# A Mamba-2 and sliding-window-attention trunk on one core: group 3's queries ahead of output block 1, the residual's scaling in the key/value block, and no transpose of probabilities on TensorE

## The chip, the cores and the metric

The kernel runs on one core of a Trainium2 chip. The metric is device time in microseconds (us) of one execution. The core's engines each work through an instruction queue of their own: TensorE (PE in the profile, its weight loads PEld), VectorE (DVE), ScalarE (ACT), GpSimd (POOL) and SyncE (SP, which here only issues transfers). They wait for each other by semaphores.

## The reference

A trunk of two layers on 256 tokens of width 2048, in float32. The first is a Mamba-2 mixer, the second an attention layer; each is followed by `LayerNorm(alpha * x + mixer(x))`. The change touches the second layer only:

```
k, v = _shared_kv(x, kv_w, kv_b, cos, sin)      # 4 heads of 64, rotary on 16 of 64
proj = x @ w_in                                  # queries (32 heads) | gate
q = rope(proj[..., :Q_WIDTH] + q_bias);  gate = proj[..., Q_WIDTH:]
s = where(valid, q k^T / 8, -inf)                # window of 128 tokens
m = max(max(s), sink)
p = exp(s - m) / (sum(exp(s - m)) + exp(sink - m))
o = (p v) * silu(gate)
out = LayerNorm(alpha * x + o @ w_out)
```

## The kernel before, in words

All large products are made in three matmuls each, from operands split into a high and a low part (`wh`, `wl` for weights, `x1H`, `x1L` for activations). Weights come in *units* of 128 x 2048, in two halves: SP loads a half into a raw buffer (`wr`, `load_half`, six buffers), ACT rounds it to `wh` (`split_half`, L163) and DVE subtracts to get `wl` (L166). Six `wh` and four `wl` buffers keep this some units ahead of PE.

The attention layer works on two halves `h` of 128 tokens and four *groups* `j` of eight heads, one key/value head each. Its stages, in the order of `B_ORDER`, are blocks of four units:

- the key/value block (L982 to L1017): `x_stat` (matmul at L975) for `h` = 0 and then, with the same four units, for `h` = 1. DVE adds the bias (L1001, L1005) and turns the keys by `rope`, POOL doubles them (L1007), PE transposes them (`ktr`, L1012).
- `q_block(j)`: 24 matmuls a unit (L975); behind the fourth unit DVE adds the bias (L1055) and does the `rope` (L960 to L965) for both halves. `qtr` transposes them on PE (L1061), and ACT copies them to `qT` (L1065).
- `gate_block(j)`: 48 matmuls a unit (L251); ACT and DVE make the gate `sg` (L1081, L1082).
- the output block `("o", j)`: `out_unit`, 24 matmuls a unit (L322 to L324); DVE adds each result to the residual `xr` (L329, L333).

Small work is hung between units. `later(n, fn)` puts `fn` on a list, and `tick()`, called behind each unit of these blocks, counts down and calls what is due; such a place on PE's queue is called a *visit* here. `tick` calls what is due in the order in which it was put on the list. `attend(j, h)` makes the scores (L1114 for `h` = 0, L1121 for `h` = 1), masks them (L1129, or ACT's copies L1134 with DVE's predicated copies L1137), takes the maximum (L1145), the exponentials on ACT (L1151) and the scale (L1157). Then the probabilities have to be turned. `turn_far` does it by a transpose of 32 x 32 blocks on DVE (L1170), copies on ACT (`moved`, L1179; ten for `h` = 0, sixteen for `h` = 1) and, for `h` = 1, two masks on DVE (`parts`, L1186). `turn_p` does it by eight transposes on PE (L1199) and four masked copies on DVE (L1205); only (j, h) = (3, 1) takes that way. `pv` makes the products with the values (L1231 for `h` = 0; L1245 and L1252 for `h` = 1), DVE multiplies by the gate (L1219), ACT and DVE split the result (L1259, L1260) for the output block.

The residual needs the first layer's normalization with gain and bias. `residual(c, h)` does it for a block of 512 columns: a multiply (L1028) and an add (L1029) on DVE, with gain and bias loaded by POOL (`load_affine`, L1023) into one pair of buffers. The eight calls are hung on visits 1 to 14 (`RES_AT`), the loads of the later blocks on `GB_AT`.

A scheduler puts the instructions of the engines in order when the program is built; where `keep_in_program_order` is asked for, it keeps the order of the code. What is built is fixed: each engine takes its queue in that order.

## Time and profile before

| what | us |
|---|---|
| median of 3 runs | 992.03 (991.72 to 992.22) |
| the profiled execution's own time | 992.29 |
| its span, first to last instruction | 990.3 |
| PE busy | 979.4 |
| DVE busy | 781.1 |
| ACT busy | 599.4 |
| POOL busy | 103.5 |
| mean granted TensorE clock | 0.999 |

The rows shown below are lines of the profile's views. A row of a timeline has start and duration in us, engine, line and operation, the tiles written and read, how many instructions are merged in it, and in brackets the engine's idle time before it and what ended that. A row of the chain has start, us and what. A row of the waits has the engine and line that waited, for whom, us in total, how often, and the longest. A row of windows has the window, its length, the busy time and count of PE, PEld, DVE, ACT and POOL, the granted clock, the DMA share and GB/s. Line numbers are those of the kernel before. The attention layer's stages run from about 661 us (key/value block) over 686 (query block 0) to 953 (last unit of output block 2), and its end to 990.

### The profile page before, as it was taken

To read this page: it belongs to the slowest core of one execution; us is meant where nothing else is said; L and a number is where in the kernel's file an instruction comes from. 1 tells how busy PE (TensorE), PEld (TensorE's weight loads), DVE (VectorE), ACT (ScalarE), POOL (GpSimd) and SP (SyncE) were. 2 spreads that over 40 slices of the span, in tenths; PEclk is the share of its full clock that TensorE was granted. 3 is DMA by queue.
4 is the path that set the end of the run, shared out by engine and by line. 5 is a ranking of instruction groups with operands and counts; after the bars stand their busy time and mean duration, and the time that the engine had idled before them with its cause. 6 is when DMAs were issued, how large, how long until landed. Compare 5 with 4: busy or idle time off the path is not lost.

```text
span 990.3 us, 18070 instructions
## 1 busy us (share of the span) xinstructions
PE 979.4 (99%) x7076; PEld 892.2 (90%) x7076; DVE 781.1 (79%) x1211; ACT 599.4 (61%) x1076; POOL 103.5 (10%) x133
## 2 busy tenths in 40 slices
PE   9999999999999999999999999999999999999998
PEld 8999989999999998999999999888898888988976
DVE  7888896867786887686787687889678878687796
ACT  7585866547646654664664664566477575674652
POOL 0001303004003002100300300302000000000003
PEclk9999999999999999999999999999999999999999
DMA  9788577575576666656657466456755557547532
GB/s 362 254 278 310 170 262 220 173 236 171 194 235 187 217 209 195 202 186 209 202 175 237 141 205 213 152 178 217 236 169 175 164 160 239 151 152 219 184 108 85
DMA packets 61557, 198.89 MB, mean 201 GB/s; under 512 B 6849, under 2 KB 11361, under 8 KB 61217
## 3 DMA queue, kind: packets, MB, share of 16 engines
q1 hardware_dynamic: 58528, 188.53, 58.9%
q0 software_dynamic: 2336, 8.69, 2.9%
q8 instruction: 55, 0.90, 0.4%
q10 hardware_dynamic: 608, 0.52, 0.2%
q14 instruction: 30, 0.24, 0.1%
HBM read 195.49 MB, written 2.23 MB: 200 GB/s over the span
## 4 chain that ended last, share of the span: by engine, by line
PE 92%; DVE 4%; ACT 2%; issue 1%; DVEq 0%; ACTq 0%
PE mm L251 50%; PE mm L975 9%; PE mm L322 9%; PE mm L323 8%; PE mm L324 8%; PE ax L630 2%; DVE wl L166 1%; ACT p L1151 1%; PE ax L606 1%; ACT pt L1179 0%; PE mm L389 0%; PE ax L589 0%; ACT wh L163 0%; PE ax L906 0%; PE ax L1114 0%
## 5 line engine op out<-in xcount | busy, mean ns | idle before, releaser
L166 DVE TENSOR_TENSOR wl<-wr,wh 128x1024 fp32r<-128x1024 f32 (+2 forms) x338 | 393.5, 1184 | 99.9 <-ACT wh L163 96.5
L163 ACT ACTIVATE wh<-wr 128x1024 fp32r<-128x1024 f32 (+2 forms) x338 | 331.2, 1010 | 154.8 <-issue 51.4
L251 PE MATMUL mm<-xH,wh 128*128 128x256 f32 x1280 | 356.1, 278 | 0.0
L251 PE MATMUL mm<-xL,wh 128*128 128x256 f32 x1280 | 354.6, 277 | 0.0
L251 PE MATMUL mm<-xH,wl 128*128 128x256 f32 x1280 | 354.5, 277 | 0.0
L251 PEld LDWEIGHTS mm<-xH,wh 128*128 128x128 f32 x1280 | 240.8, 188 | 2.0 <-issue 0.5
L251 PEld LDWEIGHTS mm<-xL,wh 128*128 128x128 f32 x1280 | 240.7, 188 | 1.0
L251 PEld LDWEIGHTS mm<-xH,wl 128*128 128x128 f32 x1280 | 240.5, 188 | 0.0
L322 PE MATMUL mm<-wh,yH 128*128 128x512 f32 x256 | 101.5, 397 | 0.0
L323 PE MATMUL mm<-wh,yL 128*128 128x512 f32 x256 | 99.9, 390 | 0.0
L324 PE MATMUL mm<-wl,yH 128*128 128x512 f32 x256 | 99.9, 390 | 0.0
L646 POOL TENSOR_TENSOR yz<-yz,z 128x256 f32<-128x256 f32 x32 | 32.5, 1024 | 468.6 <-DVE yz L641 468.6
L251 PE MATMUL mm<-x1H,wh 128*128 128x256 f32 x256 | 71.9, 281 | 0.0
L493 DVE SCALAR_TENSOR_TENSOR cv<-mm,pc,cv 128x255 f32<-128x255 f32 x144 | 68.7, 477 | 3.3 <-ACT cv L491 1.9
L251 PE MATMUL mm<-x1H,wl 128*128 128x256 f32 x256 | 71.1, 278 | 0.0
L251 PE MATMUL mm<-x1L,wh 128*128 128x256 f32 x256 | 71.1, 278 | 0.0
L975 PE MATMUL mm<-wh,x1H 128*128 128x512 f32 x160 | 63.0, 394 | 0.0
L975 PE MATMUL mm<-wl,x1H 128*128 128x512 f32 x160 | 61.9, 390 | 0.0
L975 PE MATMUL mm<-wh,x1L 128*128 128x512 f32 x160 | 60.9, 390 | 0.0
L322 PEld LDWEIGHTS mm<-wh,yH 128*128 128x128 f32 x256 | 48.1, 188 | 10.3 <-DVE z L582 0.9
L324 PEld LDWEIGHTS mm<-wl,yH 128*128 128x128 f32 x256 | 48.1, 188 | 10.1
L331 DVE SCALAR_TENSOR_TENSOR xr<-mm,r,xr 128x512 f32<-128x512 f32 x64 | 47.1, 745 | 11.7 <-PE mm L324 7.4
(226 smaller groups left out, 1373.1 us busy)
## 6 DMA issues: line engine op xcount, KB each, us to landing
wr<-in_wa SPq DMA_DIRECT2D x154, 512.0 KB, 5.1
wr<-in_wo SPq DMA_DIRECT2D x64, 512.0 KB, 4.5
wr<-in_wq SPq DMA_DIRECT2D x32, 512.0 KB, 4.0
wr<-in_wg SPq DMA_DIRECT2D x31, 512.0 KB, 4.9
wr<-in_wb SPq DMA_DIRECT2D x16, 512.0 KB, 4.7
wr<-in_wb SPq DMA_DIRECT2D x32, 256.0 KB, 3.7
rb<-rscr SPq DMA_DIRECT2D x11, 512.0 KB, 4.1
wr<-in_wkv SPq DMA_DIRECT2D x8, 512.0 KB, 5.0
```

Source lines behind the costliest of these rows:

```text
L163: m = nc.scalar.activation(h[:, sl], v, AF.Copy)
L166: m = nc.vector.tensor_tensor(l[:, sl], v, h[:, sl].bitcast(F32), ALU.subtract)
L251: m = nc.tensor.matmul(ps, a, b, start=first and i == 0, stop=last and i == 2)
L322: pinned(nc.tensor.matmul(ps, aH[:, k, hs], u.h[:, ks], start=k == 0 and add is None, stop=False), pin)
L323: pinned(nc.tensor.matmul(ps, aL[:, k, hs], u.h[:, ks], start=False, stop=False), pin)
L324: pinned(nc.tensor.matmul(ps, aH[:, k, hs], u.l[:, ks], start=False, stop=k == 3), pin)
L331: nc.vector.scalar_tensor_tensor(v, ps, rms[:, h : h + 1], v, ALU.mult, ALU.add)
L493: nc.vector.scalar_tensor_tensor(a[:, sft:], ps[:, : S - sft], w(3 - sft), a[:, sft:], ALU.mult, ALU.add)
L606: nc.tensor.transpose(ps[:, o : o + P], st.xs[i][:, c * P : (c + 1) * P], ident)
L630: nc.tensor.matmul(ps[64 * r : 64 * r + 64, cols], xd[:, c, r, :], e[:, 256:] if c else e[:, :256], start=c == 0, stop=c == 1,)
L646: nc.gpsimd.tensor_tensor(v, v, st.z[i][:], ALU.mult)
L975: m = nc.tensor.matmul(ps[:], (x1H, x1L, x1H)[i][:, kk, hs], (u.h, u.h, u.l)[i][:, ks], start=(kk, i) == (0, 0), stop=ui == 3 and (k, i) = ...
```

## The change

Five edits, all in the second layer.

1. `B_ORDER`: query block 3 stands before output block 1, which was ahead of it.
2. `turn_p` is gone. Scores (3, 1) take `turn_far` as all others do, and `attend(3, 1)` comes three visits behind `attend(3, 0)`, not one.
3. `PV_AT` and `MASK_AT` are lists per group. The query transposes are put at the head of the list (`place`), the masks too; the first product comes in the visit of the query transposes of the next group, the second in the visit of its first scores, ahead of them.
4. `residual` and `load_affine` move: the first block's gain and bias are loaded during the key/value block's first unit, the second's during its fourth, the third's and fourth's right behind each half, all in buffers of their own. Three residuals are called in the second half of the key/value block, five on visits 0 to 4.
5. In `rope` the last add, in `residual` the multiply and in `parts` both masks keep the order of the code.

Visits are counted from the first unit of query block 0. What hangs on them, before and after (turn = transpose of queries, S = scores, M = masks, V = products with the values):

```
before: 4 turn 0; 5 S00; 8 S01; 12 M01, turn 1; 13 V00 V01 S10; 16 S11; 20 M11; 21 V10 V11;
        24 turn 2; 25 S20; 28 S21; 32 M21; 33 V20 V21; 36 turn 3; 37 S30; 38 S31; 41 turn_p; 42 V30 V31
after:  4 turn 0; 5 S00; 8 S01; 12 turn 1, M01 V00; 13 V01 S10; 16 S11; 22 M11; 24 turn 2, V10;
        25 V11 S20; 28 S21; 32 turn 3, M21 V20; 33 V21 S30; 36 S31; 40 M31; 41 V30 V31
```

The diff, cut to its core:

```
-B_ORDER = [("q", 0), ("g", 0), ("q", 1), ("g", 1), ("o", 0), ("q", 2), ("g", 2), ("o", 1),
-           ("q", 3), ("g", 3), ("o", 2), ("o", 3)]
-RES_AT = [2, 3, 6, 7, 11, 12, 14, 15]
-MOVE_AT, MASK_AT = [2, 2, 3, 3], 4
-PV_AT = [[8, 5], [5, 4]]
-GB_AT = [0, 4, 8, 13]
+B_ORDER = [("q", 0), ("g", 0), ("q", 1), ("g", 1), ("o", 0), ("q", 2), ("g", 2), ("q", 3),
+           ("o", 1), ("g", 3), ("o", 2), ("o", 3)]
+MOVE_AT, MASK_AT = [2, 2, 3, 3], [4, 6, 4, 4]
+GB_AT = {0: 0, 3: 1}
+PV_AT = [[7, 5], [11, 9], [7, 5], [8, 5]]
...
-    def later(n, fn):
-        pending.append([n, fn])
+    def later(n, fn, place=None):
+        pending.insert(len(pending) if place is None else place, [n, fn])
...
+    def load_affine(c):
+        if c:
+            t = bp.tile([P, 1024], F32, tag="own" if c == 1 else "p", name=nm("gb1"), bufs=1 if c == 1 else 3)
+            gb1[c] = t[:, :512], t[:, 512:]
+        else:
+            gb1[c] = [bp.tile([P, 512], F32, tag=f"gb{i}", name=nm("gb1"), bufs=1)[:] for i in range(2)]
+        for v, n in zip(gb1[c], ("lng", "lnb")):
+            nc.gpsimd.dma_start(v, A[n][0, c * 512 : (c + 1) * 512].partition_broadcast(P))
...
+                if ui in GB_AT:
+                    load_affine(GB_AT[ui])
+            elif ui:
+                residual(ui // 3, 1 if ui == 2 else 0)
...
+        if h == 0:
+            load_affine(2)
+    load_affine(3)
+    for n in range(1, 6):
+        later(n, lambda n=n: residual((n + 2) // 2, (n + 2) % 2))
...
-            later(1, qtr)
+            later(1, qtr, h)
...
-                    nc.vector.tensor_tensor(d, t, masked(kc, 8), ALU.mult)
+                    tc.keep_in_program_order(nc.vector.tensor_tensor(d, t, masked(kc, 8), ALU.mult))
...
-                later(MASK_AT, parts)
+                later(MASK_AT[j], parts, 0)
...
-        def turn_p():
...
-        if far:
-            turn_far()
-        else:
-            later(3, turn_p)
-        later(PV_AT[j == 3][h], pv)
+        turn_far()
+        later(PV_AT[j][h], pv)
         if h == 0:
-            later(1 if j == 3 else 3, lambda: attend(j, 1))
+            later(3, lambda: attend(j, 1))
```

The built queues of the changed kernel in the stretch from scores (2, 1) on, in order (w = half a weight unit, named by block and unit; xr = output sum; S, M, V, turn as above):

```
DVE: ... S21 copies, maximum | S21 scale, w o1.1, transpose, w o1.1, w o1.2, bias and rope of query half 0,
     bias and four rope products of half 1, w o1.2, last two rope operations, w o1.3, xr, w o1.3, xr,
     first M21, gate V20, second M21, low V20, w g3.0, xr, w g3.0, xr, w g3.1, gate V21, w g3.1, low V21,
     S30 mask and maximum, xr, xr | xr, S30 scale, w g3.2, transpose, xr, w g3.2, w g3.3 (2), w o2.0, gate,
     S31 copies, w o2.0, maximum | gate, S31 scale, w o2.1, transpose, w o2.1, w o2.2, gate, gate, w o2.2,
     xr, w o2.3 (2), xr, first M31, w o3.0, second M31, ...
ACT: ... S21 exponentials, w o1.1 (2), w o1.2, 16 copies, w o1.2, w o1.3 (2), w g3.0, queries 3 (2), w g3.0,
     V20, w g3.1 (2), V21, S30 exponentials, w g3.2 (2), w g3.3 (2), 10 copies, w o2.0, gate, w o2.0,
     S31 copies, S31 exponentials, gate, w o2.1 (2), w o2.2, 8 copies, gate, 8 copies, gate, w o2.2, w o2.3 (2), ...
```

More of the change, by code (lines that the diff above doesn't have):

```diff
@@ L964, in rope @@
         nc.vector.tensor_tensor(x1, a, b, ALU.subtract)
-        nc.vector.tensor_tensor(x2, d, e, ALU.add)
+        tc.keep_in_program_order(nc.vector.tensor_tensor(x2, d, e, ALU.add))
     def x_stat(ps, h, u, ui, pin=False, last=None):
@@ L979, in x_stat, with residual @@
             pinned(m, pin)
+    gb1 = {}
+    def load_affine(c):
[6 more added lines that the diff above has]
+            nc.gpsimd.dma_start(v, A[n][0, c * 512 : (c + 1) * 512].partition_broadcast(P))
+    def residual(c, h):
+        v = xr[:, h, c * 512 : (c + 1) * 512]
+        tc.keep_in_program_order(nc.vector.tensor_tensor(v, v, gb1[c][0], ALU.mult))
+        nc.vector.tensor_tensor(v, v, gb1[c][1], ALU.add)
     kT = bp.tile([P, 4, S], F32, tag="kT", name="kT")
@@ L1017, in trunk @@
         later(2, ktr)
-    def load_affine(c):
-        for i, n in enumerate(("lng", "lnb")):
-            gb1[i] = bp.tile([P, 512], F32, tag=f"gb{i}", name=nm("gb1"), bufs=1)
-            nc.gpsimd.dma_start(gb1[i][:], A[n][0, c * 512 : (c + 1) * 512].partition_broadcast(P))
-    def residual(c, h):
-        v = xr[:, h, c * 512 : (c + 1) * 512]
-        tc.keep_in_program_order(nc.vector.tensor_tensor(v, v, gb1[0][:], ALU.mult))
-        nc.vector.tensor_tensor(v, v, gb1[1][:], ALU.add)
-    gb1 = {}
-    load_affine(0)
-    for c in range(4):
-        if c:
-            later(GB_AT[c], lambda c=c: load_affine(c))
-        for h in range(2):
-            later(RES_AT[2 * c + h], lambda c=c, h=h: residual(c, h))
+        if h == 0:
[3 more added lines that the diff above has]
+        later(n, lambda n=n: residual((n + 2) // 2, (n + 2) % 2))
     qT = {}
@@ L1099, in attend @@
         p = bp.tile([P, 1024], F32, tag="p", name=nm("p"), bufs=3)
-        far = j < 3 or h == 0
-        byhead = p[:].rearrange("p (c r b) -> p r c b" if far else "p (r c b) -> p r c b", r=8, c=4)
+        byhead = p[:].rearrange("p (c r b) -> p r c b", r=8, c=4)
         per = 512 // nk
@@ L1190, in turn_far @@
             if h:
-                later(MASK_AT, parts)
-        def turn_p():
-            for kc in range(2):
-                pts[kc] = bp.tile([P, 4, 8, 32], F32, tag=("pri", "own")[kc], name=nm("pt"), bufs=1)
-            for par in range(2):
-                pt = ax_tile()
-                for a in range(4):
-                    nc.tensor.transpose(
-                        pt[:, a * P : (a + 1) * P], p[:, (par * 4 + a) * P : (par * 4 + a + 1) * P], ident
-                    )
-                got = blocks(pt[:].rearrange("p (a q) -> p a q", a=4))
-                for kc in range(2):
-                    t = pts[kc][:].rearrange("p c r b -> p r c b")[:, par * 4 : par * 4 + 4]
-                    nc.vector.tensor_tensor(t, got, masked(kc, 4), ALU.mult)
+                later(MASK_AT[j], parts, 0)
         def pv():
```

## The prediction

> **What bounds the kernel now.** I read the page first, then who waited for whom on TensorE (PE) from 690 us on, the chain of work that ended last, and the timelines of VectorE (DVE), ScalarE (ACT) and GpSimd (POOL).

> ```profile
> PE 979.4 (99%) x7076; PEld 892.2 (90%) x7076; DVE 781.1 (79%) x1211; ACT 599.4 (61%) x1076; POOL 103.5 (10%) x133
> PE ax L1061 <- DVE qt L965: 2.0, 1, 2.0
> PE ax L1199 <- DVE p L1157: 1.7, 1, 1.7
> PE ax L1114 <- DVE o L1219: 1.3, 1, 1.3
> ```

> PE is the bound. In the attention half it waits three times, 5.0 us in all, and never for a weight. So an edit is worth something only if it takes work off PE, ends one of these waits or makes a new one. What PE's blocks take, from the chain (start, us, what):

> ```profile
> 697.41 10.90 PE mm L975 x48
> 708.31 5.46 PE mm L251 x48
> 713.77 0.87 PE ax L1061 x8
> 720.11 1.09 PE ax L1114 x16
> 863.92 1.46 PE ax L1121 x32
> 892.84 1.01 PE ax L1231 x4
> 893.85 0.86 PE ax L1245 x8
> 894.72 0.59 PE ax L1252 x8
> 944.90 1.06 PE ax L1199 x8
> 953.90 0.43 PE mm L322
> 954.33 0.23 PE mm L323
> ```

> A query or output unit is 24 matmuls, 5.45 us; a gate unit 48, 5.46. The first matmul behind a visit takes 0.43 in place of 0.23, so a visit costs 0.2 beside its own work.

> **What the change gives.** *No turn on TensorE:* eight transposes at 0.11 (0.87 for eight) go, with 0.1 of the visit's edge: 0.95. Their wait, 1.7, goes too. A wait is counted from the modelled end of the last matmul, some 0.16 behind where the next could start (0.27 for one transpose against 0.11 from start to start), so I add 0.16 to each: 1.86.

> *Residual moved.* DVE and POOL around the old and the new place:

> ```profile
> 757.06 0.68 DVE L1028 TENSOR_TENSOR xr<-xr,gb 128x512 f32<-128x512 f32 x1
> 762.13 1.22 DVE L166 TENSOR_TENSOR wl<-wr,wh 128x1024 fp32r<-128x1024 f32 x1
> 763.40 0.22 DVE L965 TENSOR_TENSOR qt<-rt 128x64 f32<-128x64 f32 x1
> 773.28 0.68 DVE L1219 TENSOR_TENSOR o<-ax,sg 128x512 f32<-128x512 f32 x1
> 675.06 1.63 POOL L1091 MEMSET pt<- 32x256 f32 x3 [11.93 <-DVE x1L L923]
> 686.12 0.42 DVE L1001 TENSOR_TENSOR kd<-mm,bias 128x256 f32<-128x256 f32 x1
> 688.68 1.93 POOL L1007 COPY kd<-kd 128x256 f32<-128x256 f32 x1 [0.98 <-DVE kd L965]
> 696.54 0.87 PE ax L1012 x8
> ```

> The wait of L1061 (2.0, so 2.16) stood behind four of DVE's multiplies and adds since the scores (0.60 each from start to start) and half a weight unit (1.13) between the last rope operations. In the new order all five are gone from there: L965 ends at 763.6 - 2.4 - 1.1 = 760.1, and PE asks at 761.6. So 2.16 goes. In its new place the scaling puts L1001 about 2 us later (part of the multiplies and adds stand ahead of it, some in gaps), so the key copy ends at 692.6; PE asks at 696.5. That, and DVE's 2 us on weights, for which PE doesn't wait, I cost at 0; without the cover it would be 2. Six loads move ahead of POOL's memset and key copies, 0.54 us of issue each by the kernel before, 3.2 in all: the 11.93 of idle time ahead of the memset hides them. On SP's queue eight loads of output block 1 change places with eight of query block 3; a load of this size lands 4 us after its issue:

> ```profile
> wr<-in_wq SPq DMA_DIRECT2D x32, 512.0 KB, 4.0
> ```

> Both blocks' loads are issued as buffers come free, three units ahead of use (16 us): 0.

> *Shared visits:* the first product of a group goes into the visit of the query turns, and the second comes ahead of the next scores. The product visits of groups 1 and 2 are no longer visits of their own: 2 x 0.2 = 0.4. For group 0 the wait of L1114 (1.3, so 1.46) shrinks: ahead of DVE's L1219 four multiplies and adds (2.4) and half a unit (1.1) go, so it stands at 773.3 - 3.5 = 769.8 and ends at 770.4; PE asks at 770.0, so 0.35 is left and 1.1 goes.

> Together: 0.95 + 1.86 + 2.16 + 0.4 + 1.1 = 6.5 us.

> **What it costs.** Group 3's queries now stand before output block 1, and scores (3,1) go the long way: DVE transpose, sixteen copies on ACT, two masks on DVE. PE takes its matmuls in program order, so it waits at the visit that comes too early. How long the path takes, from group 2 as it is:

> ```profile
> 867.77 1.17 ACT L1134 COPY p<-ax 128x256 f32<-128x256 f32 x4
> 874.98 0.21 ACT L1149 ACTIVATE sm<-sm 128x8 f32<-128x8 f32 x1 [2.97 <-DVE sm L1148]
> 881.96 6.66 ACT L1179 COPY pt<-z 32x256 f32<-32x256 f32 x16 [0.84 <-DVE z L1170]
> 868.87 2.48 DVE L1137 COPY_PREDICATED p<-cc,ax 64x128 f32<-64x128 uint32 x8
> 880.09 0.68 DVE L333 TENSOR_TENSOR xr<-xr,mm 128x512 f32<-128x512 f32 x1
> 883.55 2.35 DVE L166 TENSOR_TENSOR wl<-wr,wh 128x1024 fp32r<-128x1024 f32 x2
> 888.65 1.23 DVE L1186 TENSOR_TENSOR pt<-pt,cc 128x1024 f32<-128x1024 f32 x1 [2.15 <-ACT pt L1179]
> 890.93 1.22 DVE L1186 TENSOR_TENSOR pt<-pt,cc 128x1024 f32<-128x1024 f32 x1
> 920.60 1.28 DVE L1129 TENSOR_TENSOR p<-ax,cc 128x512 f32<-128x512 f32 x2
> 924.79 0.49 ACT p L1151 x2
> 932.47 2.90 ACT L1179 COPY pt<-z 32x256 f32<-32x256 f32 x7 [1.17 <-DVE z L1170]
> ```

> Scores at 863.92, copies from 881.96 (18.0 later), second mask at 892.15: 28.2 us. From start to start DVE takes 1.13 for half a weight unit (L166) or a mask, 0.60 for an output sum (L333); ACT 0.415 a copy, 1.0 for a weight half. Now the changed kernel's queues in their new order; 0 is where PE starts scores (2,1).

> 1. Copies start at 18.04 less three output sums (1.8), which are no longer there, and with one weight half more (1.13): 17.4. Sixteen take until 24.0. Behind them on ACT stands the second half of output block 1's third unit, and behind that on DVE the last two rope operations of the queries (3, second half): 24.0 + 1.1 + 1.2 + 0.35 = 26.7. PE asks at 1.46 + 96 matmuls (21.8) + 0.2 + 0.44 = 23.9. **New wait: 2.8.**
> 2. DVE then works off what gathered before it gets to scores (3,0): six weight halves (6.9), four output sums (2.4), two masks (2.3), the products and their low halves (2.4): 40.7.
> 3. From L1129 to the copies 11.9 as at 920.60 to 932.47, by the new order 11.6: 52.3.
> 4. Ten copies (4.15); on ACT a weight unit and a gate before the scores (3,1), which PE made at about 54: 58.7. Masked copies 2.5 and half a unit 1.1 on DVE, the maximum and small ones 1.8: exponentials at 64.4. From there to the copies 7.7 (924.79 to 932.47 in group 3 now): 72.1.
> 5. Sixteen copies with two gates among them (7.4), a weight half on ACT (1.1): 80.6. In DVE's order now stand: half a unit, sum, two halves, sum, mask, half, mask: 4 x 1.13 + 2 x 0.60 + 1.13 + 1.22 = 8.1: **88.7**.

> PE without a wait would ask for the second mask at: 216 matmuls at 0.227 (49.0), 192 gate matmuls at 0.114 (21.9), small blocks 1.46 + 0.8 + 1.0 + 1.5 + 1.1 + 1.46 + 1.0 = 8.3, edges 1.0: **80.2**. So 8.5 us of waiting arise between, however they are split (2.8 at the turns, about 0.7 for accumulators that DVE reads late, 5 at the products of group 3). These hops have an error of some 2 us together. The nearest rows bound it: at least 0 (a path of 28.2 as in group 2 would fit into the 29.9 that PE leaves from scores (3,1) to its products), at most 11 (with two more weight halves ahead).

> Sum without the clock: 992.29 - 6.5 + 8.5 = 994.3 against the profiled execution, 0.26 above the median of 992.03; so 994.0.

> *The clock:*

> ```profile
> 983.57 1.99 PE L1342 MATMUL ax<-t,dg 128*128 128x256 f32 x6
> 985.00:988.00 3.00, 0.56 (x2) 0.00 (x0) 2.03 (x4) 0.69 (x2) 0.00 (x0) 1.00 0.79 293
> 988.00:990.30 2.30, 0.00 (x0) 0.00 (x0) 0.00 (x0) 0.00 (x0) 0.00 (x0) 0.51 0.22 74
> 1.00 2.96 PE L371 MATMUL ax<-zero 128*128 128x512 bf16 x7 [1.00 <-DVE zero L359]
> 4.96 0.34 PE L251 MATMUL mm<-xL,wh 128*128 128x256 f32 x1
> ```

> The last matmul ends at 985.6, and from 988 the granted clock is 0.51: under 2.5 us of rest were enough. At the start six and a half widths of 512 take 2.96, 0.46 each against 0.23: half speed, until the matmuls quicken at about 4.96, 4 us after the first. So a drop costs at most half of 4, 2.0, and at least 0. A rest of 5 us is likely to bring one; the waits of 2 us of before brought none. I take 1.5, nearer the row with the drop. **995.5.** A drop at the first wait costs nothing, since the path above sets the later end.

> [...]

> **Rivals.** (a) *Masks of (3,1) in time, faster.* If DVE is not as far behind as step 2 says, the path of (3,1) takes group 2's 28.2 against 29.9, and only 2.8 at the turns stays: 992.0 - 6.5 + 2.8 = 988.3. It decides once the second mask ends before 82. For it: group 2 was just as full and made it. Against: now output sums and eight halves stand between, and scores (3,0) are only three units ahead. (b) *Neither wait:* 985.5. (c) *Half of it:* a path shorter by 2 to 4 us, no drop: 990 to 993. (d) *Waits, but the clock stays:* 994.0; for it, rests are split by the accumulators. (e) *More late than this:* weights behind the copies on ACT too, 998 and above; against it, weights come 7 us and more ahead in most units, by the lack of any wait for them.

> **How the numbers follow.** Forecast with the drop 0.36, (d) 0.2, (a) 0.19, (b) 0.07, (c) 0.11, (e) 0.07. The likeliest has its own range of 993.5 to 998; with (a) it reaches down to 987, with (d) and (c) between; (b) and (e) mostly stay out: 987.0 to 998.5. About 0.2%, 2 us, is what can be told from no change: faster than 990.0 is (a) and (b), 0.25; within 990.0 to 994.0 (c) and a half of (d), 0.21; slower 0.54.

> **What would show it.** L1199 gone, L1061's wait of group 1 gone, L1114's under 0.5. New: PE waiting at the turns of query block 3 for the last rope operation, 2 to 3 us, behind L166 and the sixteen copies; and at the second product of group 3 for the mask, 4 to 6 us; granted clock under 1.00 just behind it. No wait of PE in the key/value block. I am wrong if DVE ends the masks of (3,1) before PE asks, or if PE waits for weights.

## The result, and the profile after

| | us, median | lowest to highest | ratio to before |
|---|---|---|---|
| before | 992.21 | 991.72 to 993.79 (5 runs) | |
| after | 1001.89 | 1000.41 to 1003.89 (5 runs) | 1.0096, 95% interval 1.008 to 1.0112 |

The change costs about 9.7 us. The profiled execution of the changed kernel took 1001.16, its span is 999.4. Line numbers are from here on those of the changed kernel unless said otherwise: the key copy on GpSimd (POOL) is L1028, the residual's multiply and add are L996 and L997, the transposes of the keys L1033, the copy of the turned keys on ScalarE L1036, the query transposes L1067, the masks L1191, the matmuls of query and key units L974, those of output units L321 to L323, group products with both halves of the keys L1236, rope L959 to L964, the weight halves L162 (ScalarE, ACT) and L165 (VectorE, DVE).

TensorE (PE) from 660 us on, "who waited for whom" (what waited, what for: us in all, times, longest):

```profile
PE ax L1236 <- DVE pt L1191: 3.9, 1, 3.9
PE ax L1033 <- POOL kd L1028: 3.3, 1, 3.3
PE ax L1067 <- DVE qt L964: 2.8, 1, 2.8
PE mm L321 <- DVE sm L1151: 0.4, 1, 0.4
```

The three waits of before are gone (those at L1061 for group 1, at L1114 and at L1199 in that kernel's lines). Three others stand in their place, and a small one for accumulators. The first and the third row were forecast, with about 5 and 2.8; the second, 3.3 us at the transposes of the keys, was forecast not to be there. The chain of what ended last, by stretches around the three (start, us, what):

```profile
693.89 6.46 POOL kd L1028
...
700.39 0.66 PE ax L1033 x4
701.04 7.11 PE mm L974 x24
...
892.57 0.15 DVE qt L964
...
892.85 1.08 PE ax L1067 x4
...
953.47 1.23 DVE pt L1191
...
954.84 1.98 PE ax L1236 x8
```

Behind the first wait 24 matmuls take 7.11 us; before, 48 took 10.90, so 24 should take 5.45. They are slow for 3.4 us of it, from 701.69 on. The stretches of the granted clock, by windows (window: length, then busy us of each engine with the number of its instructions, granted clock, DMA share, GB/s):

```profile
698.28:701.69 3.41, 1.30 (x8) 1.17 (x9) 1.80 (x3) 0.61 (x2) 2.06 (x1) 1.00 0.84 276
701.69:705.10 3.41, 3.41 (x10) 2.62 (x9) 2.41 (x3) 0.93 (x1) 0.00 (x0) 0.50 0.56 185
...
889.42:892.83 3.41, 0.66 (x5) 0.37 (x4) 1.62 (x4) 3.37 (x5) 0.00 (x0) 1.00 0.04 14
892.83:896.25 3.42, 3.40 (x9) 1.48 (x10) 3.42 (x5) 3.19 (x6) 0.00 (x0) 0.50 0.76 206
...
950.86:954.27 3.41, 0.05 (x2) 0.00 (x0) 3.41 (x4) 2.92 (x3) 0.00 (x0) 1.00 0.90 258
954.27:957.69 3.42, 2.85 (x16) 1.16 (x16) 3.42 (x6) 0.15 (x2) 0.00 (x0) 0.50 0.70 227
```

Each of the three waits is followed by 3.41 us at half the clock. Half of what PE works in it is lost: 1.7, 1.7 and, as PE still rests for 0.57 of the third, 1.4 us. The kernel before had no such stretch: its granted clock was 1.00 from 5 to 985 us.

Where the first wait comes from stands in the timelines of GpSimd, VectorE and ScalarE (start, us, engine, line, operation; in brackets idle time before and what ended it):

```profile
678.89 0.72 POOL L1028 COPY kd<-kd 128x256 f32<-128x256 f32 x1 [2.08 <-DVE kd L964]
...
690.72 9.62 POOL L1028 COPY kd<-kd 128x256 f32<-128x256 f32 x1 [0.98 <-DVE kd L964]
```

```profile
690.46 0.19 DVE L964 TENSOR_TENSOR kd<-rt 128x32 f32<-128x32 f32 x1
690.56 0.69 DVE L996 TENSOR_TENSOR xr<-xr,gb 128x512 f32<-128x512 f32 x1
691.17 1.22 DVE L165 TENSOR_TENSOR wl<-wr,wh 128x1024 fp32r<-128x1024 f32 x1
...
699.12 0.96 DVE L165 TENSOR_TENSOR wl<-wr,wh 128x768 fp32r<-128x768 f32 x1
702.66 1.23 DVE L165 TENSOR_TENSOR wl<-wr,wh 128x1024 fp32r<-128x1024 f32 x1 [2.58 <-ACT wh L162]
```

```profile
701.08 0.59 ACT L1036 COPY kT<-ax 128x512 f32<-128x512 f32 x1 [3.00 <-PE ax L1033]
701.57 1.06 ACT L162 ACTIVATE wh<-wr 128x1024 fp32r<-128x1024 f32 x1
```

The second key copy starts at 690.72, just when the prediction had it (692.6 less 1.93). But it takes 9.62 us, not 1.93, and ends at 700.34, 0.26 behind VectorE's last instruction (699.12 + 0.96 = 700.08). VectorE had run without a gap all that time, on instructions that read two inputs from SBUF. The kernel before shows the same thing on a smaller scale, in its own lines (its key copy is L1007; the second one's row, 688.68 with 1.93, stands in the prediction):

```profile
678.77 1.33 POOL L1007 COPY kd<-kd 128x256 f32<-128x256 f32 x1 [2.08 <-DVE kd L965]
...
688.52 1.23 DVE L166 TENSOR_TENSOR wl<-wr,wh 128x1024 fp32r<-128x1024 f32 x1
689.66 0.69 DVE L1028 TENSOR_TENSOR xr<-xr,gb 128x512 f32<-128x512 f32 x1
690.39 0.77 DVE L1029 TENSOR_TENSOR xr<-xr,gb 128x512 f32<-128x512 f32 x1
```

That copy ended at 690.61. The border between L166 and L1028, at 689.7, had not let it in; the first gap, the 0.04 us between multiply and add (689.66 + 0.69 = 690.35 to 690.39), did, and it ended 0.26 behind the gap's start. In the changed kernel weight pieces stand between multiplies and adds, and there is no such gap.

And the three engines closed a circle: VectorE ran dry because ScalarE's next weight half (L162 at 701.57) stood behind the copy of the turned keys (L1036), which waited for PE's transposes, which waited for GpSimd's copy, which had to wait until VectorE ran dry.

### The profile page after: what moved, and what is told of

The parts are those of the page before. It is cut to its first block, busy times and chain, and to the rows that moved or that the text cites. A ratio compares the mean times of both kernels' runs of the same rounds, so it can differ in the third digit from the quotient of the medians.

```text
span 999.4 us, 18069 instructions
## 1 busy us (share of the span) xinstructions
PE 983.4 (98%) x7068; PEld 892.4 (89%) x7068; DVE 783.2 (78%) x1210; ACT 606.3 (61%) x1092; POOL 109.1 (11%) x133
## 4 chain that ended last, share of the span: by engine, by line
PE 89%; DVE 4%; ACT 2%; issue 2%; DMA 1%; POOL 1%; DVEq 0%; SPq 0%; ACTq 0%; POOLq 0%
PE mm L250 51%; PE mm L974 8%; PE mm L321 8%; PE mm L322 8%; PE mm L323 8%; PE ax L629 2%; ACT pt L1184 1%; DVE wl L165 1%; DMA wr<-in_wb 1%; PE ax L605 1%; DVE p L1142 1%; POOL kd L1028 1%; ACT p L1156 1%; ACT wh L162 1%; PE ax L1236 1%
## 5 line engine op out<-in xcount | busy, mean ns | idle before, releaser
L165 DVE TENSOR_TENSOR wl<-wr,wh 128x1024 fp32r<-128x1024 f32 (+2 forms) x338 | 392.7, 1183 | 102.8 <-ACT wh L162 101.0
L162 ACT ACTIVATE wh<-wr 128x1024 fp32r<-128x1024 f32 (+2 forms) x338 | 331.5, 1010 | 148.8 <-PE mm L250 53.3
L321 PE MATMUL mm<-wh,yH 128*128 128x512 f32 x256 | 101.4, 396 | 0.0
L322 PE MATMUL mm<-wh,yL 128*128 128x512 f32 x256 | 99.8, 390 | 0.0
L323 PE MATMUL mm<-wl,yH 128*128 128x512 f32 x256 | 99.7, 389 | 0.0
L974 PE MATMUL mm<-wh,x1H 128*128 128x512 f32 x160 | 63.4, 396 | 0.0
L974 PE MATMUL mm<-wl,x1H 128*128 128x512 f32 x160 | 62.4, 393 | 0.0
L974 PE MATMUL mm<-wh,x1L 128*128 128x512 f32 x160 | 61.6, 394 | 0.0
L321 PEld LDWEIGHTS mm<-wh,yH 128*128 128x128 f32 x256 | 48.1, 188 | 10.3 <-DVE z L581 1.0
L323 PEld LDWEIGHTS mm<-wl,yH 128*128 128x128 f32 x256 | 48.1, 188 | 10.2
## 6 DMA issues: line engine op xcount, KB each, us to landing
wr<-in_wa SPq DMA_DIRECT2D x154, 512.0 KB, 5.0
wr<-in_wo SPq DMA_DIRECT2D x64, 512.0 KB, 4.4
wr<-in_wq SPq DMA_DIRECT2D x32, 512.0 KB, 4.6
wr<-in_wg SPq DMA_DIRECT2D x31, 512.0 KB, 4.8
wr<-in_wb SPq DMA_DIRECT2D x16, 512.0 KB, 4.3
rb<-rscr SPq DMA_DIRECT2D x11, 512.0 KB, 4.1
wr<-in_wkv SPq DMA_DIRECT2D x8, 512.0 KB, 4.7
```

What stands on the lines that cost most here:

```text
L162: m = nc.scalar.activation(h[:, sl], v, AF.Copy)
L165: m = nc.vector.tensor_tensor(l[:, sl], v, h[:, sl].bitcast(F32), ALU.subtract)
L321: pinned(nc.tensor.matmul(ps, aH[:, k, hs], u.h[:, ks], start=k == 0 and add is None, stop=False), pin)
L322: pinned(nc.tensor.matmul(ps, aL[:, k, hs], u.h[:, ks], start=False, stop=False), pin)
L323: pinned(nc.tensor.matmul(ps, aH[:, k, hs], u.l[:, ks], start=False, stop=k == 3), pin)
L974: m = nc.tensor.matmul(ps[:], (x1H, x1L, x1H)[i][:, kk, hs], (u.h, u.h, u.l)[i][:, ks], start=(kk, i) == (0, 0), stop=ui == 3 and (k, i) = ...
```

## The experiments

**1. The key copy on ScalarE.** Theory A: GpSimd is kept out of SBUF by VectorE's gapless run.

```
-        nc.gpsimd.tensor_copy(kd[:, :, 1, :], kd[:, :, 0, :])
+        (nc.scalar.copy if h else nc.gpsimd.tensor_copy)(kd[:, :, 1, :], kd[:, :, 0, :])
```

> The changed kernel with one edit: the second key copy (L1028, second half of the rows) runs on ScalarE instead of GpSimd; nothing else moves. Theory A (GpSimd's read of SBUF is locked out while VectorE runs instructions with two SBUF inputs without a gap, since the moved residual fills VectorE's gaps): the copy then ends by about 692, PE's 3.3 us wait at the visit of the keys goes, and so does the half-clock stretch of 3.41 us behind it (1.7 us): 1001.9 - 3.5 - 1.7 = 996.7 us. Rival B (the keys themselves are late, because the residual pushes VectorE's bias and rope back): the copy starts as late as before and PE still waits 3 us or more: 1001 to 1002. Rival C (the wait is hidden by the later waits anyway, because the masks of group 3 set the end): the wait goes, the later ones grow by as much: 1000 or above.

Measured: 997.12 (996.44 to 997.48). The wait and the half-clock stretch behind it are gone (mean clock of the profiled run 0.997, 0.995 in the changed kernel's), 4.8 us in all; the other two waits stand as they were (4.0 and 2.9). That fits A. The keys were not late (B), and the later waits did not take the gain back (C).

**2. The residual later, the copy left on GpSimd.**

```
     for n in range(1, 6):
-        later(n, lambda n=n: residual((n + 2) // 2, (n + 2) % 2))
+        later(n + 2, lambda n=n: residual((n + 2) // 2, (n + 2) % 2))
```

> The changed kernel with one edit: the five residual steps that stand in query block 0 come two visits later (third to seventh visit in place of first to fifth); the three in the key/value block and the copy on GpSimd stay. Theory A (GpSimd locked out by a gapless VectorE): VectorE has gaps again behind the key's rope, the 9.6 us copy falls to 1 to 2 us, PE's wait and the clock drop behind it go: about 996.7, plus 0 to 1.5 if the later residual now delays the first queries' rope: 996 to 998.5. Rival (the copy is slow because of what GpSimd itself does: the loads and the bias issue in its queue): copy still 9 to 10 us, time 1001 to 1002.

Measured: 997.04 (996.33 to 998.18). The copy takes 5.41, not 1 to 2, since VectorE now does five weight pieces without a gap; but it ends before PE asks. GpSimd's row, and VectorE's:

```profile
691.23 5.41 POOL L1028 COPY kd<-kd 128x256 f32<-128x256 f32 x1 [0.97 <-DVE kd L964]
```

```profile
691.08 4.70 DVE L165 TENSOR_TENSOR wl<-wr,wh 128x1024 fp32r<-128x1024 f32 x5
695.69 0.68 DVE L996 TENSOR_TENSOR xr<-xr,gb 128x512 f32<-128x512 f32 x1
696.41 0.77 DVE L997 TENSOR_TENSOR xr<-xr,gb 128x512 f32<-128x512 f32 x1
```

The copy ends at 696.64. The first gap in VectorE's run is the 0.04 us between L996 and L997 (695.69 + 0.68 = 696.37 to 696.41): L997 adds to what L996 has just written. The copy ends 0.27 behind that gap's start, and L997 took 0.77 in place of 0.68. So what lets the copy in need not be an idle engine: a gap of 0.04 us was enough, here as in the kernel before.

**3. Group 3's second products one visit later.**

```
-PV_AT = [[7, 5], [11, 9], [7, 5], [8, 5]]
+PV_AT = [[7, 5], [11, 9], [7, 5], [8, 6]]
```

> The changed kernel with one edit: the second value products of group 3 one visit later (six visits behind their scores in place of five). Theory A (the long way of the masks is what the second product waits for, 3.9 us, and half clock for 3.41 us follows): the wait and the drop go and nothing takes their place, as the last output block asks for the result about 11 us later: 1001.9 - 4.1 - 1.7 = 996.1. Rival B (the work behind is late anyway, so a wait appears at the start of the last output block or in the final normalization): 1000 or above. Rival C (wait goes, clock drop stays for another reason): 997.8.

Measured: 995.26 (994.04 to 1001.02, 8 runs). The wait of 3.9 is gone and nothing takes its place; the work behind it has about 10 us to spare (the second half's result is ready at 966.2; the last output block asks for it behind its four units of the first half, at about 976, an estimate from 48 matmuls of 0.23), so B falls. Its runs spread by 7 us, and they follow the mean granted clock: 994.04 and 994.09 at 1.0, 1001.02 at 0.993.

**4. The sixteen copies of scores (2,1) behind the weight unit.**

```
-                later(MOVE_AT[c], lambda c=c: moved(c))
+                later(4 if (j, h) == (2, 1) else MOVE_AT[c], lambda c=c: moved(c))
...
-                later(MASK_AT[j], parts, 0)
+                later(MASK_AT[j], parts, None if j == 2 else 0)
```

> The changed kernel with one edit: the sixteen copies of scores (2,1) are issued one to two visits later, so that on ScalarE the second half of output block 1's third unit stands ahead of them in place of behind them, and on VectorE both rope chains of query block 3 run behind that unit without waiting for it. Theory A (the 2.8 us wait at the turns of query block 3 stands behind that half unit, as the prediction's step 1 says, and half clock for 3.41 us follows): the wait falls to 0 to 0.4, the drop goes: 1001.9 - 2.9 - 1.7 = 997.3 if the long wait at group 3's products stays as it is. Rival B (that wait is on the same path as the later one: the masks of (3,1) come no earlier, so the later wait grows by what this one loses, as the prediction's sum had it): only the clock is won: about 1000. Rival C: the masks of (2,1) come too late for their products and a new wait of 1 to 3 us takes the place: 1000 to 1002.

Measured: 1001.8 (1000.78 to 1003.5): nothing won. PE from 890 to 960:

```profile
PE ax L1236 <- DVE pt L1191: 6.6, 2, 3.3
PE ax L1067 <- DVE qt L964: 0.2, 1, 0.2
```

The 2.8 us at the turns fell to 0.2, as expected, so it did stand behind that half unit on ScalarE. But the masks of (2,1) now came late for their own products: L1236 waits twice, 3.3 us each, once for group 2 and once for group 3. Rival C was right. The waits add to as much as before, 10.5 us against 10.4: the time was not saved, it was moved along the same queue.

**5. The residual's move alone, on the kernel before.** The functions load_affine and residual and their calls as in the changed kernel, all else as before.

> The kernel before with one part of the change: the residual scaling and its loads move into the key/value block, everything else as before. As the prediction priced it: the wait of L1061's group 1 (2.16) goes and the move costs nothing: 992.2 - 2.2 = 990.0. By the theory of the locked-out copy: VectorE runs gapless behind the key's rope, the second key copy on GpSimd takes about 9 us, PE waits 3.3 us there (3.5 in all), and a half-clock stretch follows if enough of the wait falls into one window of the clock (1.7 or 0): 992.2 - 2.2 + 3.5 + 0 to 1.7 = 993.5 to 995.2.

Measured: 997.92 (995.07 to 1000.8). It makes the kernel slower by itself: ratio 1.0052 (1.0033 to 1.0072). The copy takes 9.63 us and PE waits 3.3, as in the changed kernel. L1061's wait (L1068 in this file) did not go either; it is 3.3 in place of 2.0. VectorE's queue shows why: the multiplies and adds are gone from there, but the first mask of scores (0,1) now stands between the two halves' rope operations and waits 2.02 us for ScalarE's copies. In the changed kernel it stands behind them. So the prediction's 2.16 took the fixed order too; the move alone does not win it. The profiled run (995.07) has no half-clock stretch behind the wait at the keys, though it is as long as in the changed kernel:

```profile
695.61:699.02 3.41, 1.61 (x10) 1.12 (x8) 3.41 (x6) 1.62 (x3) 3.41 (x1) 1.00 0.82 290
699.02:702.44 3.42, 1.91 (x11) 1.65 (x12) 1.19 (x2) 1.21 (x2) 1.46 (x1) 1.00 0.86 296
```

Here the wait falls across the border of two windows of 3.41 us, 1.8 and 1.5 us of rest. In the changed kernel 2.1 us of rest lay in one window (698.28 to 701.69, PE busy 1.30). The five runs of this kernel show what the stretches cost: 995.07 and 995.36 at a mean clock of 1.0, 997.92 at 0.996, 999.63 and 1000.8 at 0.994.

**6. The waits filled.**

```
+        for _ in range(n):     # 12, 10 and 16, ahead of the three waiting visits
+            pinned(nc.tensor.matmul(t[:], x1H[:, 0, :P], x1H[:, 0:2, :], start=True, stop=True), True)
```

> The changed kernel with idle work put into PE's three waits: ahead of the transposes that wait for the second key copy, for the last rope operation of query block 3 and ahead of the products that wait for the mask stand 12, 10 and 16 matmuls of 128x512 (0.23 us each: 2.7, 2.3 and 3.6 us) on data that is long there, into an accumulator that nobody reads. They change no output and shorten no wait of the data. Theory A (the half-clock stretches come from the idle time alone and cost about 1.7 us each): all three go, the waits stay as long in total: 1001.9 - 5.1 = 996.8. Rival B (the slow matmuls behind the waits have another cause): 1001 to 1002. Rival C (the matmuls take time themselves because the waits are shorter than they look): 1000 or above with the waits' rows gone.

Measured: 1000.02 (999.88 to 1000.34), with a mean clock of 1.0 in all four runs: no half-clock stretch is left, so the rest was their cause. The gain is 1.9, not 5.1, and PE still waits 2.3, 0.9 and 0.5 us behind the dummies. The three visits take 18.5 us, from their first matmul to the next weight's, as long as in the changed kernel, where two of them ran partly at half clock: 5.31 us of dummies and rest stand ahead of the second transposes of the keys where the wait was 3.3. GpSimd's row tells why (the copy is L1033 here):

```profile
690.65 11.37 POOL L1033 COPY kd<-kd 128x256 f32<-128x256 f32 x1 [0.97 <-DVE kd L964]
```

VectorE had two more instructions without a gap in this build, and the copy went on to 702.02, 1.7 us later, 0.27 behind the start of the next gap (0.03 us, again between a multiply and its add). For the price of a stretch this run is of little use; it is told for the 11.37.

**7 and 8. Waits taken out together.** The seventh kernel has the edits of 1 and 3. The eighth has those of 1 and 4, PV_AT = [[7, 5], [11, 9], [7, 6], [9, 6]].

> The changed kernel with the edits of the first and the third experiment together: key copy on ScalarE, second products of group 3 one visit later. If the two waits and the half-clock stretches behind them are separate, the gains add: 1001.9 - 4.8 - 6.6 = 990.5, with the 2.9 us wait at the turns of query block 3 left, with or without a half-clock stretch (1.7). If they are not, 995 or above.

> The changed kernel with all three waits taken out: key copy on ScalarE; the sixteen copies of scores (2,1) behind the weight unit as in the fourth experiment, but with the second products of group 2 one visit later (six behind their scores), where the masks are ready; both products of group 3 one visit later, in one visit. If the prediction's gains are there as priced (6.5 us) and only waits hid them: 992.2 - 6.5 + 0.2 for a visit that is no longer shared = 985.9, with no wait over 0.5 us on PE in the attention half. If the gains were priced too high, or the work put off meets the last output block: 988 to 992.

Measured: 990.68 (ratio 0.9984, 0.9975 to 0.9993) and 989.95 (0.9979, 0.997 to 0.9987). The two gains add, 990.5 forecast. Both kernels are a little faster than the one before, by 0.2%. The eighth missed its 985.9: its profiled run, the longest of its eleven (992.77), has small waits of 2.4 us in all, among them 0.9 for the products' halves at the first unit of the last output block.

**9. A probe for the copy's wait and for the clock.** One GpSimd copy of 128x256 beside different runs of VectorE, then blocks of matmuls with gaps. This probe and the next each ran once.

> A probe that computes nothing of the reference (its output is zeros). Part one: VectorE writes 128x64, on which one GpSimd copy of 128x256 waits; VectorE goes on, twice each, with nothing; four and eight multiplies of 128x1024 with both inputs in SBUF and outputs of their own; four, one of 128x512 with an input in PSUM, four; eight with an input in PSUM; eight with both inputs in SBUF that all write the same tile (so each waits for the one ahead of it). If GpSimd is let in only when VectorE leaves a gap or takes an input from PSUM: the copy takes under 1 us with nothing and beside inputs from PSUM, about 4.5 and 9 us beside four and eight (1.13 each from start to start), about 5 in the mixed stream, 1 to 2.5 in the chained one. Rival (the lock is held for the one running instruction only, and GpSimd comes next): 1 to 2 us in every stream. Part two: blocks of 30 to 41 matmuls of 128x512 with a gap between two blocks of about 0.6, 1.2, 1.9, 2.4, 2.9 and 4 us, twelve of each, so that they fall differently on the windows of 3.41 us in which the granted clock changes. If a window with about 1.9 us or more of idle time halves the clock of the next: no half-clock stretch behind gaps up to 1.8, behind some of those of 2 to 3.4, behind all of 4. Rival (only a gap of 3.4 us counts): behind those of 4 alone.

GpSimd's copies beside nothing, eight multiplies, the mixed run, inputs from PSUM and the chained run (the one beside four took 1.26):

```profile
16.93 0.40 POOL L66 COPY kd<-kd 128x256 f32<-128x256 f32 x1 [16.48 <-DVE kd L65]
...
23.93 1.27 POOL L66 COPY kd<-kd 128x256 f32<-128x256 f32 x1 [4.28 <-DVE kd L65]
34.01 1.27 POOL L66 COPY kd<-kd 128x256 f32<-128x256 f32 x1 [8.82 <-DVE kd L65]
44.70 0.40 POOL L66 COPY kd<-kd 128x256 f32<-128x256 f32 x1 [9.42 <-DVE kd L65]
50.28 1.26 POOL L66 COPY kd<-kd 128x256 f32<-128x256 f32 x1 [5.18 <-DVE kd L65]
```

Theory A in its first form fell: beside eight gapless instructions the copy took 1.27, not 9. It ended at 25.20, some 0.27 behind the end of the first of the eight (an estimate: it started at 23.71, and one of this size took 1.22 in experiment 10), while the run went on to 33.07. Beside inputs from PSUM it took 0.40, as beside nothing. So two inputs from SBUF did hold it up (1.27 against 0.40), but a gapless run was not enough for 9 us.

For the clock: behind 24 gaps of 0.97 and 1.50 us no half-clock stretch, behind 5 of 12 gaps of 2.10, 5 of 12 of 2.64, 11 of 12 of 3.8 to 4.2. Sorted by the rest in one window of 3.41 us, of those that ran at full clock: none of 166 with less than 2.05 us of rest was followed by half clock, 7 of 10 with 2.05 to 2.3, all 13 above. Half clock came behind 5 of the 12 gaps of 2.10 too, so the rival falls.

**10. What the first probe lacked.**

> A second probe, which computes nothing of the reference either (zeros). In the first one a GpSimd copy got in behind the one VectorE instruction that was running, 1.26 us in all, beside any gapless stream; in the changed kernel the first key copy did so too (0.72 us), and only the second stood for 9.62 us. What is different there: a load (the queries' bias) was issued on GpSimd's queue 1.5 us ahead of it; and VectorE's stream is mixed (512 wide in place, 1024 wide with another output type). The probe tries a strided copy like the kernel's (128x4x64), twice each: beside eight equal multiplies; beside a stream mixed like the kernel's; the same two with a load issued on GpSimd's queue one VectorE instruction earlier (1.2 us); and with the load four and nine instructions earlier (4.6 and 10 us). Theory A2 (a load in the making on GpSimd's queue keeps the copy out until VectorE leaves a gap): about 1.3 us without a load, the length of the stream (6.5 to 9 us) with a load issued 1.2 us ahead, and 1.3 again with the load 10 us ahead. Theory A3 (the mix of VectorE's instructions does it): long beside the mixed stream with and without a load, 1.3 beside the equal one. If all are 1.3, neither is it, and what keeps the second copy out stays open.

GpSimd, with the load one, one (mixed run), four and nine instructions ahead; and VectorE around the third:

```profile
47.18 1.26 POOL L81 COPY kq<-kq 128x256 f32<-128x256 f32 x1 [0.56 <-DVE kq L80]
...
58.53 0.73 POOL L81 COPY kq<-kq 128x256 f32<-128x256 f32 x1 [0.57 <-DVE kq L80]
...
71.16 9.21 POOL L81 COPY kq<-kq 128x256 f32<-128x256 f32 x1 [3.97 <-DVE kq L80]
...
91.78 9.21 POOL L81 COPY kq<-kq 128x256 f32<-128x256 f32 x1 [9.65 <-DVE kq L80]
```

```profile
66.27 4.62 DVE L65 TENSOR_TENSOR m<-f 128x1024 f32<-128x1024 f32 x4
70.81 0.22 DVE L80 TENSOR_TENSOR kq<-f 128x64 f32<-128x64 f32 x1
70.95 9.16 DVE L65 TENSOR_TENSOR m<-f 128x1024 f32<-128x1024 f32 x8
80.41 0.23 DVE L89 TENSOR_TENSOR kd<-kq,f 128x64 f32<-128x64 f32 x1 [0.29 <-POOL kq L81]
```

The 9 us are there, but not where A2 or A3 had them. A load 1.2 us ahead leaves 1.26, a load 10 us ahead gives 9.21; the mixed run gives 0.73. What sets the long cases apart is how long VectorE had run without a gap before the copy asked: with one big instruction ahead the copy ended at 48.44, some 0.26 behind the end of the one that was running (an estimate: it started at 46.96, and the one ahead took 1.22); with four (4.6 us) or nine no border let it in until the run ended (80.11; the copy ended at 80.37). The rows shown came out the same in both rounds of the probe. Its very first copy (128x128) had nine instructions ahead and no load on the way, and took 9.16 as well; in the second round, where VectorE had a gap 0.4 us before it asked, the same copy took 1.22. So the load is not needed. The changed kernel fits: ahead of the first key copy (0.72) VectorE had a gap 0.4 us earlier, ahead of the second (9.62) none since its last read of PSUM, 1.9 us and eight instructions before. Whether time or number decides, and where the border lies, wasn't tried.

**11. One read of PSUM in the changed kernel.** The sum behind the rope writes a tile that nobody reads:

```
         nc.gpsimd.tensor_copy(kd[:, :, 1, :], kd[:, :, 0, :])
+        if h:
+            idle = bp.tile([P, 4, P], F32, tag="qT", name="idle", bufs=2)
+            tc.keep_in_program_order(nc.vector.tensor_tensor(idle..., ps[:, :256], kvb[:, :256], ALU.add))
```

> The changed kernel with one more VectorE instruction: right behind the rope of the second half of the keys stands a sum of 128x256 with one input from PSUM (0.42 us), whose output nobody reads. Nothing is taken away; the copy stays on GpSimd and the residual stays where the change put it. Theory A (GpSimd gets its read of SBUF only while VectorE has no second SBUF input in flight, and in a run of such instructions that has lasted a while no boundary between two lets it in): the copy runs beside the one read of PSUM and ends within about 1 us in place of 9.62; PE's wait at the keys and the half-clock stretch behind it go: about 997, as with the copy on ScalarE (997.1). Rival (only an idle VectorE lets it in, or VectorE's added work is what counts): the copy stays over 8 us, 1002 or above.

GpSimd and VectorE at that place:

```profile
690.98 0.40 POOL L1028 COPY kd<-kd 128x256 f32<-128x256 f32 x1 [11.10 <-DVE kd L964]
```

```profile
690.84 0.41 DVE L1032 TENSOR_TENSOR idle<-mm,bias 128x256 f32<-128x256 f32 x1
691.18 0.75 DVE L996 TENSOR_TENSOR xr<-xr,gb 128x512 f32<-128x512 f32 x1
691.85 1.21 DVE L165 TENSOR_TENSOR wl<-wr,wh 128x1024 fp32r<-128x1024 f32 x1
```

Measured: 997.39 (996.47 to 999.02), as with the copy on ScalarE. With 0.41 us more work on VectorE the copy takes 0.40 in place of 9.62. This shows the cause in the kernel itself: it is not how much VectorE has to do, but that every instruction takes its second input from SBUF without a break.

**12. The best version.** The eighth with PV_AT = [[7, 5], [11, 9], [7, 6], [8, 6]].

> The version with all three waits out (989.95) with the first product of group 3 back in its earlier visit, the second one visit later as before. There PE waited 0.57 and 0.35 us for the products' low and high halves at the first unit of the last output block, and 0.7 us for accumulators that VectorE read late. If those come from both products falling into one visit: 989.95 - 0.9 to 1.6 + 0.2 for the visit of its own = 988.6 to 989.3. If not: 990 or above.

Measured: 988.38 (988.26 to 989.19), ratio 0.9959 (0.9946 to 0.9971): 4.0 us under the kernel before, whose median beside it was 992.43, and 13.5 under the changed one by the medians. All waits of PE from 660 us on:

```profile
PE mm L321 <- DVE sg L1088: 0.9, 2, 0.7
PE mm L321 <- DVE sm L1151: 0.4, 1, 0.4
PE ax L1067 <- DVE qt L964: 0.2, 1, 0.2
```

The gain agrees with the prediction's prices as a sum: 6.5, less two visits that are no longer shared (0.4), less these waits (1.5, and 0.16 for each of four), is 4.0. The interval of the ratio is 2.9 to 5.4 us, so it doesn't check each price.

## Why the prediction was right and wrong

**Direction and mechanism of the order: right.** "No turn on TensorE", L1061's wait and the shared visits came together about as priced (experiment 12's sum, within its interval); one by one they were not measured, and the move of the residual alone did not end L1061's wait (experiment 5). L1114's wait went altogether, 0.35 more than said.

**The long path: right, nearly to the hop.** Scores (2,1) start at 866.08. The last rope operation ended 26.6 behind that (26.7 said), the second mask of (3,1) at 954.69, 88.6 behind (88.7 said); each hop between came within 0.4 us. (Step 4's items add to 64.1, not the 64.4 written; measured were 64.07. The chances of (a) and (b) add to 0.26, not 0.25.) The wait at the turns is 2.8 (2.8 said), accumulators 0.4 (0.7), the products 3.9 (5): the half-clock stretch behind the turns made PE 1.7 us late and so shortened the last wait. That is what "a drop at the first wait costs nothing" meant, and it held.

**The clock: one of three stretches priced.** The prediction took 1.5 for a stretch behind the long wait; it was 1.4. The one behind the turns cost nothing in the end, and the one behind the keys it did not have. In the changed kernel's trace each of the three lasts 3.41 us, and they start on one grid (701.69, 892.83 and 954.27 lie 56 and 18 times 3.413 apart); in experiment 2 one lasted twice that (948.71 to 955.53). In the changed kernel 2.11 us of rest within one window (698.28 to 701.69) were enough.

**The step that failed: "That, and DVE's 2 us on weights, for which PE doesn't wait, I cost at 0; without the cover it would be 2."** The residual's move was priced by VectorE's time alone. The key copy was put at its old 1.93 us, as if that were its work; nothing was made of the 1.33 that the same copy takes 10 us earlier. It was the sign: alone the copy took 0.40 (experiment 9), and the rest was waiting for VectorE, then too. In place of the 0 stand 3.5 us of wait and 1.7 of half clock. The sum with what was measured: 994.3 (against the profiled execution, without the clock) + 1.4 + 3.5 + 1.7 = 1000.9, against 1001.16; that is closer than its terms, with some 2 us of error in the path alone, could promise. With the copy on ScalarE (997.12) or let in by the read of PSUM (997.39) the kernel lies within the 993.5 to 998 that the prediction gave its likeliest case. None of the rivals had it; the highest, weights late on ScalarE, came out at a like time by another way, and no wait for a weight is in the trace.

The probe's rows speak against this step: the copy took 1.26 or 1.27 beside VectorE's two inputs from SBUF and 0.40 beside reads of PSUM. With the wait of these rows the copy would have cost one VectorE instruction more, about 1.2 us by the rows of L165 (an estimate), and been hidden by the 3.9 that it had to spare (692.6 to 696.5). The traces show more than that wait: 9.62 in the changed kernel, 11.37 in experiment 6 and 9.21 in experiment 10, over eight instructions and more, where VectorE's run was already some instructions old (eight since the last read of PSUM in the changed kernel, four or nine big ones in experiment 10).

**What stays open.** Why a border between two instructions let GpSimd in early in a run (1.26, experiment 10) and not later (9.21): no run here shows it. How the 1.9 us that the filled waits won (experiment 6) divide between the clock and the longer wait for the copy was not separated.

## What to carry to other kernels

Before work is put into another engine's idle time, ask what that idle time was doing: in the kernel before, GpSimd's copy ended 0.26 us behind a gap of 0.04 us in VectorE's run and took 1.93 us; without such a gap it took 9.62. The same copy took 0.40 to 11.37 us in the runs here, by what VectorE ran beside it; two ways out worked in this kernel, the copy on ScalarE and one instruction that reads PSUM beside it. A wait that is taken out can come back further along the same queue: taking out the turns' wait alone won nothing, while those at the keys and at the last products were worth 4.8 and 6.6 us, each taken out alone.
